# Latent norms inside the loop over tiles, and seven gate pairs a layer as block products with their last multiply on GpSimd

## The chip, the cores and the metric

The kernel runs on one core of one Trainium2 chip. The metric is device time in microseconds; the kernel before takes 1251.12 us (median of 3 runs, 1249.96 to 1251.63). A core has five engines with a queue each: TensorE (PE in the rows; its weight loads, PEld, run beside its matmuls), VectorE (DVE), ScalarE (ACT), GpSimd (POOL) and SyncE (SP), which here only issues DMA transfers.

## The reference

Two layers (DEPTH 2) on a sequence of 512 tokens of width 1024. A layer is a mixing part with four groups of attention heads, and a SwiGLU feed-forward part of inner width 2816:

```
z = rmsnorm(x, g_pre_mix) @ w_in                      # one projection for all four groups
z_moba, z_fox, z_fg, z_cq, z_ckv, z_kr, z_dil = split(z)
c_q  = rmsnorm(z_cq,  g_mla_q)                        # 192 wide   } the "latent norms"
c_kv = rmsnorm(z_ckv, g_mla_kv)                       # 128 wide   }
q_c = c_q @ w_mla_q_up ;  kv = c_kv @ w_mla_kv_up     # then rotary parts, attention
...                                                   # MoBA, FoX and dilated attention
x = x + rmsnorm(concat(heads) @ w_out, g_post_mix)
h = rmsnorm(x, g_pre_ffn)
f = silu(h @ w_gate) * (h @ w_up)
x = x + rmsnorm(f @ w_down, g_post_ffn)
```

All is float32. The kernel writes each operand as a sum of two parts (hi and lo), and one product is three matmuls (`mm3`: hi·hi, hi·lo, lo·hi, lines 197 to 199).

## The kernel before

Tokens are handled as four tiles of 128 (`NT`). The order of the instructions on each engine is set by the framework's scheduler from the order of the code, its dependences and its own costs; only the opening is written out by hand. Each engine then runs its list strictly in that order, and a list that waits holds up all that stands behind it. SP's list is the list of weight loads: each waits until one of five buffers `wraw` is free again.

**Start of the mixing part** (lines 540 to 665). A loop over the four tiles multiplies out the FoX values (`ps_v`) and the latent columns (`ps_lat`), and ScalarE copies the latter to `lat[t]` (L555). Then come FoX's q and k projections (`ps_qk`, 24 matmuls of 512 columns each). Only behind them in the code stand the gains' transfer (`gqkv`, L591 and L592, on SP's queue) and a second loop over the tiles with the latent norms: ScalarE sums the squares (L599, L600), GpSimd makes the factor r (L602 to L604), VectorE multiplies `lat` by r and gain (L605, L606), TensorE transposes three pieces (`cq0T`, `cq1T`, `ckvT`, L608 to L610). The transposed latents are split in hi and lo (`sp_hi`, `sp_lo`, L614, L615; `q_stk`, L620 and L621) and multiplied with the up weights, a tile at a time (`ps_qup`, `ps_kvup`), the results are put in natural order, and `natT` transposes them by heads (L670). `ps_cum` and `cumT` belong to FoX's forget gates, `ps_s` is a block of attention scores.

**Feed-forward part** (`ffn`). The 22 blocks j of 128 columns of w_gate and w_up are handled in pairs. Pair 0 is done in halves of the tokens. All ten other up pairs, and the gate pairs that start at j = 4, 8, 12, 16 and 20, go through `two_blocks`: the pair's weights as a 2 by 2 matrix of blocks, times h as a 2 by 2 matrix, in 7 products of blocks in place of 8. A product (`ps<-...`) is 12 matmuls of 256 columns, so a pair takes 84. It costs sums of weight blocks (`wsum`, `combine`, L886), a split of each sum or block (`whi` on ScalarE, `wlo` on VectorE, L880 and L881) and adds of the results (L898). The other gate pairs (2, 6, 10, 14, 18) are done directly (`ps_g`): 2 blocks of 24 matmuls of 512 columns, 48 in all, each block with two splits (L168, L173). When a pair's gate and up are there, silu (L936) and the multiply gate·up follow, in two instructions of 128x512 on VectorE (L944). Then f times w_down (`ps_d`) runs to the end of the layer.

Two names that the text uses: g4 is the gate pair that starts at block 4, u4 the up pair there.

Of the kernel before, what the change touches and what calls it, by code (L numbers as in the profile page):

```python
# [9 lines left out]
F32 = mybir.dt.float32  # L10
F32R = mybir.dt.float32r
I32 = mybir.dt.int32
AF = mybir.ActivationFunctionType
ALU = mybir.AluOpType
PSUM = bass.MemoryType.PSUM

P = 128
# [6 lines left out]
EPS = 1e-6  # L24
# [13 lines left out]
L_CQ, L_CKV, L_KR = 4, 196, 324  # L38
# [43 lines left out]
def decoder(ctx, tc, x, positions, w_in, b_forget, g_mla_q, w_mla_q_up, g_mla_kv, w_mla_kv_up,  # L82
            w_out, g_pre_mix, g_post_mix, w_gate, w_up, w_down, g_pre_ffn, g_post_ffn, consts, out):
    nc = tc.nc
# [4 lines left out]
    small = ctx.enter_context(tc.tile_pool(name="small", bufs=8))  # L89
# [5 lines left out]
    def bank(pool, name):  # L95
        return pool.tile([P, 512], F32, name=name, tag=pool.name)
# [4 lines left out]
    def R(dt, name):  # L101
        return keep.tile([P, 512], dt, name=name, tag="ring", bufs=NR)

    def T(dt, name):
        return keep.tile([P, 512], dt, name=name, tag="temp", bufs=NTMP)

    def H(name):
        return keep.tile([P, 512], F32, name=name, tag="part", bufs=NPART)
# [21 lines left out]
    mhalf = keep.tile([P, 2], F32, name="mhalf")  # L130
# [29 lines left out]
    def weights(src, shape, into=None):  # L160
        raw = wp.tile([P] + shape, F32, name="wraw", tag="wraw", bufs=WRAW)
        if into is None:
            hi = wp.tile([P] + shape, F32R, name="whi", tag="whi", bufs=WSPL)
            lo = wp.tile([P] + shape, F32R, name="wlo", tag="wlo", bufs=WSPL)
        else:
            hi, lo = into
        nc.sync.dma_start(raw, src)
        nc.scalar.copy(hi, raw)  # L168
        chunk_no[0] += 1
        if pool_share[0] and chunk_no[0] % pool_share[0] == 0:  # L170
            nc.gpsimd.tensor_tensor(lo, raw, f32(hi), op=ALU.subtract)
        else:
            nc.vector.tensor_tensor(lo, raw, f32(hi), op=ALU.subtract)  # L173
        return hi, lo
# [21 lines left out]
    def mm3(ps, a_hi, a_lo, b_hi, b_lo, start, stop):  # L196
        nc.tensor.matmul(ps, a_hi, b_hi, start=start, stop=False)  # L197
        nc.tensor.matmul(ps, a_hi, b_lo, start=False, stop=False)  # L198
        last_mm[0] = nc.tensor.matmul(ps, a_lo, b_hi, start=False, stop=stop)  # L199
# [74 lines left out]
    def mixing(l, h_in, in_slots, out_slots, w_first):  # L274
        def hh(k, ts=slice(0, S)):
            return h_in[0][k // 4][:, k % 4, ts]

        def hl(k, ts=slice(0, S)):
            return h_in[1][k // 4][:, k % 4, ts]
# [80 lines left out]
        def proj_qk(c0, rotary):  # L360

            passes = {}
            q = {}

            w = {}

            def fetch(j):
                w[j] = fetch_T(c0 + P * (2 * (j % 2) + j // 2))

            def step_q(i):  # L370
                ps = yield from proj_T(w[2 * i])
                q[i] = q_pair(rope(ps, 0.125), 1.0) if rotary else q_pair(ps, 0.125)

            def step_k(i):
                ps = yield from proj_T(w[2 * i + 1])
                for j, (kh, kl) in enumerate(k_pair(rope(ps, 1.0) if rotary else ps)):
                    passes[2 * i + j] = [(q[i][j], kh), (q[i][j], kl)]

            return passes, [(lambda j=j: fetch(j), lambda j=j: (step_k if j % 2 else step_q)(j // 2), 5.2) for j in range(4)]
# [156 lines left out]
        def window(col):  # L536
# [5 lines left out]
        lat = [latq[:, t, :] for t in range(NT)]  # L542
# [2 lines left out]
        lat_lo = [slot(s, F32R, "lat_lo") for s in out_slots[1:3]]  # L545
        wl = [weights(w_in[l, k * P:(k + 1) * P, C_LAT:C_LAT + N_LAT], [N_LAT],
                      into=(lat_hi[:, k, :], lat_lo[k // 4][:, k % 4, 0:N_LAT])) for k in range(KD)]
        for t in range(NT):
            for _ in steps[t][1]():
                pass  # L550
            ps = bank(ps_mm, "ps_lat")
            ts = slice(t * P, (t + 1) * P)
            for k in range(KD):
                mm3(ps[:, 0:N_LAT], hh(k, ts), hl(k, ts), *wl[k], k == 0, k == KD - 1)
            nc.scalar.copy(lat[t][:, 0:N_LAT], ps[:, 0:N_LAT])  # L555

        fox_passes, fox_qk = proj_qk(C_FOX, False)
        run(fox_qk[:1])
# [27 lines left out]
        if l == 0:  # L586
            with tc.issue_after(normed[0].ins), tc.issue_after(normed[1].ins):
                rope_tables()
        gains_lat = R(F32, "gqkv")
        gq, gkv = gains_lat[:, 0:192], gains_lat[:, 192:320]  # L590
        nc.sync.dma_start(gq, g_mla_q[l:l + 1, :].broadcast_to([P, 192]))  # L591
        nc.sync.dma_start(gkv, g_mla_kv[l:l + 1, :].broadcast_to([P, P]))  # L592
        jk = T(F32, "jk")
        pq0, pq1 = bank(ps_t, "cq0T"), bank(ps_t, "cq1T")
        pkv = bank(ps_s, "ckvT")
        for t in range(NT):
            ss = small.tile([P, 2], F32, name="ss2", tag="ss2")
            zq, zkv = lat[t][:, L_CQ:L_CKV], lat[t][:, L_CKV:L_KR]
            nc.scalar.activation(jk[:, 0:192], zq, AF.Square, accum_out=ss[:, 0:1])  # L599
            nc.scalar.activation(jk[:, 192:320], zkv, AF.Square, accum_out=ss[:, 1:2])  # L600
            r = small.tile([P, 2], F32, name="r2", tag="r2")
            nc.gpsimd.tensor_scalar(r[:, 0:1], ss[:, 0:1], 1.0 / 192, EPS, op0=ALU.mult, op1=ALU.add)  # L602
            nc.gpsimd.tensor_scalar(r[:, 1:2], ss[:, 1:2], 1.0 / 128, EPS, op0=ALU.mult, op1=ALU.add)
            nc.gpsimd.tensor_tensor(r, r, mhalf, op=ALU.pow)  # L604
            nc.vector.scalar_tensor_tensor(zq, zq, r[:, 0:1], gq, op0=ALU.mult, op1=ALU.mult)  # L605
            nc.vector.scalar_tensor_tensor(zkv, zkv, r[:, 1:2], gkv, op0=ALU.mult, op1=ALU.mult)  # L606
            ts = slice(t * P, (t + 1) * P)
            nc.tensor.transpose(pq0[:, ts], lat[t][:, L_CQ:L_CQ + P], ident)  # L608
            nc.tensor.transpose(pq1[0:64, ts], lat[t][:, L_CQ + P:L_CKV], ident)
            nc.tensor.transpose(pkv[:, ts], zkv, ident)  # L610
# [193 lines left out]
    def ffn(l, xt, h, turns, f_slots, after):  # L804
# [5 lines left out]
        def w_of(src, j, into=(None, None)):  # L810
            cs = slice(j * P, (j + 1) * P)
            return [weights(src[l, 4 * i * P:4 * (i + 1) * P, cs].rearrange("(k p) c -> p k c", p=P), [4, P], into=into[i])
                    for i in range(2)]
# [81 lines left out]
        def two_blocks(src, j, d1, d2):  # L895

            def add(to, a, b):
                nc.vector.tensor_tensor(to, a, b, op=ALU.add)  # L898

            c11, c12, c21, c22 = [d[:, s] for d in (d1, d2) for s in half]  # L900
            a11 = raw_of(src, j, 0)
            a21, a22 = raw_of(src, j + 1, 0), raw_of(src, j + 1, 1)
            a12 = raw_of(src, j, 1)
            p1 = product(ps_mm, split_w(a11), "11")
            nc.scalar.copy(c12, p1)
            s1 = combine(a21, a22, ALU.add)
            p5 = product(ps_s, split_w(s1), "T1")
            nc.scalar.copy(c22, p5)
            p2 = product(ps_o, split_w(a12), "21")
            add(c11, p2, c12)  # L910
            s2 = combine(s1, a11, ALU.subtract)
            p6 = product(ps_mm, split_w(s2), "T2")
            add(c12, p6, c12)
            s3 = combine(a11, a21, ALU.subtract)
            p7 = product(ps_t, split_w(s3), "T3")
            add(c21, p7, c12)
            s4 = combine(a12, s2, ALU.subtract)
            add(c12, c12, c22)
            add(c22, c22, c21)
            p3 = product(ps_s, split_w(s4), "22")  # L920
            add(c12, p3, c12)
            p4 = product(ps_t, split_w(a22), "T4")
            add(c21, p4, c21)

        for j in range(KF):
            if j < 2:
                (pg, _), (pu, _) = halves[2 * j:2 * j + 2]
            elif j - j % 2 in (4, 8, 12, 16, 20):
                if j % 2 == 0:
                    two_blocks(w_gate, j, fq[j], fq[j + 1])  # L930
                pg = fq[j]
            else:
                wg, pg = w_of(w_gate, j), bank(ps_mm, "ps_g")
                block(pg, wg, slice(0, 512))
            f = fq[j]
            nc.scalar.activation(f, pg, AF.Silu)  # L936
            if j < 2:
                nc.vector.tensor_tensor(f, f, pu, op=ALU.mult)
            elif j % 2 == 1:
                u = H("u1"), H("u2")  # L940
                two_blocks(w_up, j - 1, *u)
                for i in range(2):
                    f = fq[j - 1 + i]
                    nc.vector.tensor_tensor(f, f, u[i], op=ALU.mult)  # L944

        tail = 4
        gpost = gain(g_post_ffn, l)
# [20 lines left out]
        for t in range(NT):  # L968
# [4 lines left out]
            ss = small.tile([P, 2], F32, name="ssp", tag="ssp")  # L973
            for c in range(2):
                jk = T(F32, "jk3")
                square_mean(jk, acc[t][c], ss[:, c:c + 1])
                nc.vector.tensor_tensor(y[c], acc[t][c], gpost[c], op=ALU.mult)
            r = row_rstd(ss)
# [26 lines left out]
    with tc.manual_schedule(engines={mybir.EngineType.Activation, mybir.EngineType.DVE, mybir.EngineType.Pool}):  # L1005

        st, tr = {}, {}
        for o in "s0 a0 w0 w1 t0 s1 w2 w3 a1 s2 t1 a2 s3 t2 a3 t3".split():
            t = int(o[1])
# [50 lines left out]
```

## Time and profile before

| | |
|---|---|
| median of 3 runs | 1251.12 us |
| profiled execution: time / span | 1253.86 / 1252.0 us |
| TensorE busy | 1218.8 us (97%) |
| its weight loads | 1075.3 us (86%) |
| VectorE busy | 888.2 us (71%) |
| ScalarE busy | 667.4 us (53%) |
| GpSimd busy | 219.5 us (18%) |
| chain that ended last | TensorE 82%, VectorE 6%, ScalarE 4%, DMA 3% |
| granted TensorE clock | 0.995 |

How to read it: the profiled execution is one run of its own, 2.74 us above the median of the three. Matmuls are pipelined, so a matmul's row shows 0.28 us although the next starts 0.12 us after it; what a stretch of matmuls takes is read from start to start. The chain is followed backwards from the last instruction, at each step to what released it.

### The profile page before, as it was taken

How to read it: one execution, taken by the hardware profiler on the slowest of the kernel's cores; microseconds unless marked ns; L12 is line 12 of the kernel's file. 1: busy time of each engine (PE TensorE's matmuls, PEld its weight loads, DVE VectorE, ACT ScalarE, POOL GpSimd, SP SyncE). 2: the span in 40 equal slices, each digit the busy share in tenths (PEclk: the TensorE clock that was granted, in tenths of full speed). 3: DMA queues.
4: the chain of work that ended last, by engine and by line, in shares of the span. 5: the costliest groups of instructions: out<-in, count | busy, mean ns of one | idle time of the engine just before them, and what ended most of it. 6: DMA issues, size and time to landing. Idle time of an engine off the chain costs nothing.

```text
span 1252.0 us, 20776 instructions
## 1 busy us (share of the span) xinstructions
PE 1218.8 (97%) x7404; PEld 1075.3 (86%) x7404; DVE 888.2 (71%) x1801; ACT 667.4 (53%) x1453; POOL 219.5 (18%) x305
## 2 busy tenths in 40 slices
PE   8999999989999999999999999999999999999997
PEld 7878877779999999888787888778899999998886
DVE  6876877787988888533466778677789887893334
ACT  6676766754544445333356767576554544453332
POOL 3213334343000000000131324423430000000001
PEclk9999999999999999999999999999999999999999
DMA  7321242521433333433432222434223333333321
GB/s 230 75 60 43 63 122 65 166 68 35 120 102 108 104 108 93 136 93 101 133 112 74 59 57 65 107 94 135 68 60 111 116 104 110 103 110 118 95 93 73
DMA packets 158059, 121.67 MB, mean 97 GB/s; under 512 B 9090, under 2 KB 133122, under 8 KB 157956
## 3 DMA queue, kind: packets, MB, share of 16 engines
q1 hardware_dynamic: 151908, 111.55, 30.5%
q10 hardware_dynamic: 6048, 8.80, 2.6%
q8 instruction: 58, 0.95, 0.3%
q14 instruction: 45, 0.37, 0.1%
HBM read 111.93 MB, written 4.19 MB: 93 GB/s over the span
## 4 chain that ended last, share of the span: by engine, by line
PE 82%; DVE 6%; ACT 4%; DMA 3%; issue 2%; POOL 2%; ACTq 0%; SPq 0%; DVEq 0%; POOLq 0%
PE ps L197 8%; PE ps L199 8%; PE ps L198 8%; PE ps_d L197 6%; PE ps_d L198 6%; PE ps_d L199 6%; PE ps_g L198 4%; PE ps_g L197 3%; PE ps_g L199 3%; PE ps_s L454 3%; PE ps_qk L197 2%; PE ps_qk L199 2%; PE ps_qk L198 2%; PE pT L478 2%; PE ps_out L199 1%
## 5 line engine op out<-in xcount | busy, mean ns | idle before, releaser
L173 DVE TENSOR_TENSOR wlo<-wraw,whi 128x512 fp32r<-128x512 f32 x209 | 158.3, 766 | 133.2 <-ACT whi L168 131.1
L168 ACT CAST whi<-wraw 128x512 fp32r<-128x512 f32 (+1 forms) x228 | 138.5, 620 | 177.2 <-PE ps_d L199 121.0
L880 ACT CAST whi<-wsum 128x512 fp32r<-128x512 f32 x120 | 74.3, 620 | 133.4 <-DVE wsum L886 49.7
L197 PE MATMUL ps<-sum,whi 128*128 128x256 f32 x480 | 135.3, 282 | 0.0
L198 PE MATMUL ps<-sum,whi 128*128 128x256 f32 x480 | 135.2, 282 | 0.0
L199 PE MATMUL ps<-sum,wlo 128*128 128x256 f32 x480 | 135.1, 281 | 0.0
L240 POOL TENSOR_SCALAR rstd<-ssp 128x1 f32<-128x1 f32 x16 | 6.4, 398 | 641.6 <-ACT jk L236 641.5
L197 PE MATMUL ps_d<-whi,fh 128*128 128x512 f32 x288 | 112.2, 390 | 0.0
L199 PE MATMUL ps_d<-whi,fl 128*128 128x512 f32 x288 | 112.1, 389 | 0.0
L198 PE MATMUL ps_d<-wlo,fh 128*128 128x512 f32 x288 | 112.0, 389 | 0.0
L469 POOL TENSOR_SCALAR pr<-pr,den 128x128 f32<-128x128 f32 (+3 forms) x128 | 73.7, 591 | 188.2 <-DVE den L466 161.5
L199 PE MATMUL ps<-h,wlo 128*128 128x256 f32 x360 | 101.8, 283 | 0.0
L197 PE MATMUL ps<-h,whi 128*128 128x256 f32 x360 | 101.7, 282 | 0.0
L198 PE MATMUL ps<-h,whi 128*128 128x256 f32 x360 | 101.6, 282 | 0.0
L197 PEld LDWEIGHTS ps<-sum,whi 128*128 128x128 f32 x480 | 91.8, 191 | 0.0
L198 PEld LDWEIGHTS ps<-sum,whi 128*128 128x128 f32 x480 | 91.8, 191 | 0.0
L199 PEld LDWEIGHTS ps<-sum,wlo 128*128 128x128 f32 x480 | 91.7, 191 | 0.0
L198 PE MATMUL ps_g<-h,whi 128*128 128x512 f32 (+1 forms) x224 | 81.5, 364 | 5.8 <-DVE h L231 5.8
L881 DVE TENSOR_TENSOR wlo<-wsum,whi 128x512 fp32r<-128x512 f32 x120 | 80.9, 683 | 8.5 <-ACT whi L880 7.7
L197 PE MATMUL ps_g<-h,whi 128*128 128x512 f32 (+1 forms) x224 | 81.3, 363 | 1.0 <-ACT h L231 1.0
L199 PE MATMUL ps_g<-h,wlo 128*128 128x512 f32 (+1 forms) x224 | 81.0, 362 | 0.0
L880 ACT CAST whi<-wraw 128x512 fp32r<-128x512 f32 x90 | 55.8, 619 | 40.8 <-PE ps L198 28.1
(317 smaller groups left out, 3500.6 us busy)
## 6 DMA issues: line engine op xcount, KB each, us to landing
wraw<-in_w_gate_dram SPq DMA_DIRECT2D x88, 256.0 KB, 3.5
wraw<-in_w_up_dram SPq DMA_DIRECT2D x88, 256.0 KB, 3.1
wraw<-in_w_down_dram SPq DMA_DIRECT2D x88, 256.0 KB, 2.8
wraw<-in_w_in_dram SPq DMA_DIRECT2D x72, 256.0 KB, 3.1
wraw<-in_w_out_dram SPq DMA_DIRECT2D x32, 256.0 KB, 2.7
xt<-in_x_dram SPq DMA_DIRECT2D x16, 256.0 KB, 3.3
rope_b<-rope_a ACTq DMA_DIRECT2D x64, 64.0 KB, 2.0
wraw<-in_w_in_dram SPq DMA_DIRECT2D x16, 178.0 KB, 3.6
```

The costliest lines, as they stand in the source:

```text
L168: nc.scalar.copy(hi, raw)
L173: nc.vector.tensor_tensor(lo, raw, f32(hi), op=ALU.subtract)
L197: nc.tensor.matmul(ps, a_hi, b_hi, start=start, stop=False)
L198: nc.tensor.matmul(ps, a_hi, b_lo, start=False, stop=False)
L199: last_mm[0] = nc.tensor.matmul(ps, a_lo, b_hi, start=False, stop=stop)
L240: nc.gpsimd.tensor_scalar(r, ss[:, 0:1], ss[:, 1:2], EPS, op0=ALU.add, op1=ALU.add)
L454: nc.tensor.matmul(ps[:, 0:w], a if a.shape[-1] == P else a[:, qt * P:(qt + 1) * P], b[:, 0:w], start=i == 0, stop=i == n - 1)
L469: nc.gpsimd.tensor_scalar(p, p, den[:, t - qa:t - qa + 1], 1.0, op0=ALU.mult, op1=ALU.mult)
L478: nc.tensor.transpose(pt[:, i * P:(i + 1) * P], pr[:, offs[qt] + kt * P:offs[qt] + (kt + 1) * P], ident)
L880: nc.scalar.copy(hi, raw)
L881: nc.vector.tensor_tensor(lo, raw, f32(hi), op=ALU.subtract)
```

## The change

Two things. First, the transfer of the latent gains and the norms of a tile (squares, r, multiply) move from the second loop into the first, behind that tile's copy to `lat[t]`; the transposes stay where they were in the code. Second, the gate pairs done as products of blocks are now 4, 6, 10, 12, 16, 18 and 20 (direct are left 2, 8 and 14), and in these seven pairs GpSimd does the multiply gate·up in place of VectorE.

```diff
+        gains_lat = R(F32, "gqkv")
+        gq, gkv = gains_lat[:, 0:192], gains_lat[:, 192:320]
+        nc.sync.dma_start(gq, g_mla_q[l:l + 1, :].broadcast_to([P, 192]))
+        nc.sync.dma_start(gkv, g_mla_kv[l:l + 1, :].broadcast_to([P, P]))
+        jk = T(F32, "jk")
         for t in range(NT):
...
             nc.scalar.copy(lat[t][:, 0:N_LAT], ps[:, 0:N_LAT])
+            ss = small.tile([P, 2], F32, name="ss2", tag="ss2")
+            zq, zkv = lat[t][:, L_CQ:L_CKV], lat[t][:, L_CKV:L_KR]
+            nc.scalar.activation(jk[:, 0:192], zq, AF.Square, accum_out=ss[:, 0:1])
+            nc.scalar.activation(jk[:, 192:320], zkv, AF.Square, accum_out=ss[:, 1:2])
+            r = small.tile([P, 2], F32, name="r2", tag="r2")
+            nc.gpsimd.tensor_scalar(r[:, 0:1], ss[:, 0:1], 1.0 / 192, EPS, op0=ALU.mult, op1=ALU.add)
+            nc.gpsimd.tensor_scalar(r[:, 1:2], ss[:, 1:2], 1.0 / 128, EPS, op0=ALU.mult, op1=ALU.add)
+            nc.gpsimd.tensor_tensor(r, r, mhalf, op=ALU.pow)
+            nc.vector.scalar_tensor_tensor(zq, zq, r[:, 0:1], gq, op0=ALU.mult, op1=ALU.mult)
+            nc.vector.scalar_tensor_tensor(zkv, zkv, r[:, 1:2], gkv, op0=ALU.mult, op1=ALU.mult)
...
-            elif j - j % 2 in (4, 8, 12, 16, 20):
+            elif j - j % 2 in (4, 6, 10, 12, 16, 18, 20):
...
-                    nc.vector.tensor_tensor(f, f, u[i], op=ALU.mult)
+                    (nc.gpsimd if j - 1 in (4, 6, 10, 12, 16, 18, 20) else nc.vector).tensor_tensor(f, f, u[i], op=ALU.mult)
```

The same lines that are added to the first loop are removed from the second. The lists of the engines change as follows (line numbers behind the moved lines grow by one, or by their new place).

TensorE, layer 0, at the twelve transposes of the latents. Before, they stand near the end of FoX's k projection, three matmuls of it (`ps_qk`) still behind or between them:

```order
L199 MATMUL ps_qk<-h,wlo 128x512
L608 MATMUL cq0T<-cst,lat 128x128
L609 MATMUL cq1T<-cst,lat 64x128
L608 MATMUL cq0T<-cst,lat 128x128
L609 MATMUL cq1T<-cst,lat 64x128
L610 MATMUL ckvT<-cst,lat 128x128
L197 MATMUL ps_qk<-h,whi 128x512
L610 MATMUL ckvT<-cst,lat 128x128
L198 MATMUL ps_qk<-h,whi 128x512
```

Now, between the q projection's 24 matmuls and the k projection's 24:

```order
L199 MATMUL ps_qk<-h,wlo 128x512
L609 MATMUL cq0T<-cst,lat 128x128
L610 MATMUL cq1T<-cst,lat 64x128
L611 MATMUL ckvT<-cst,lat 128x128
L609 MATMUL cq0T<-cst,lat 128x128
L610 MATMUL cq1T<-cst,lat 64x128
L611 MATMUL ckvT<-cst,lat 128x128
```

All twelve transposes have moved ahead of the k projection; the first `ps_qup` stands right behind it. The place is the same in layer 1.

SP's list of transfers in layer 0; before, the gains come behind the weights of q, k and the up projections, and two of the loads of the next values:

```order
L167 DMA wraw<-in_w_in_dram 128x356 x3
L566 DMA bf<-in_b_forget_dram 128x4
L167 DMA wraw<-in_w_in_dram 128x356 x5
L167 DMA wraw<-in_w_in_dram 128x4x128 x4
L167 DMA wraw<-in_w_mla_q_up_dram 128x384
L182 DMA wraw<-in_w_mla_q_up_dram 64x384 x2
L167 DMA wraw<-in_w_mla_kv_up_dram 128x512
L167 DMA wraw<-in_w_in_dram 128x4x128 x4
L566 DMA bf<-in_b_forget_dram 128x4
L167 DMA wraw<-in_w_in_dram 128x2x256 x2
L591 DMA gqkv<-in_g_mla_q_dram 128x192
L592 DMA gqkv<-in_g_mla_kv_dram 128x128
```

Now:

```order
L167 DMA wraw<-in_w_in_dram 128x356 x3
L550 DMA gqkv<-in_g_mla_q_dram 128x192
L551 DMA gqkv<-in_g_mla_kv_dram 128x128
L581 DMA bf<-in_b_forget_dram 128x4
L167 DMA wraw<-in_w_in_dram 128x356 x5
L167 DMA wraw<-in_w_in_dram 128x4x128 x4
```

They moved ahead of five of the eight latent weight loads, in layer 1 to just behind the eighth.

GpSimd's list in the feed-forward part of layer 0; the first rows (`b`, sums of h) open that part, and before, the list then goes on with the norms at the end of the layer:

```order
L851 TENSOR_TENSOR b_3555<-h 128x512
L851 TENSOR_TENSOR b_3563<-h 128x512
L240 TENSOR_SCALAR rstd<-ssp 128x1
L241 TENSOR_TENSOR rstd<-rstd,mhalf 128x1
```

Now, with the multiplies of pair 4 (its up tiles are u_3942 and u_3943), pair 6 and so on between:

```order
L852 TENSOR_TENSOR b_3555<-h 128x512
L852 TENSOR_TENSOR b_3563<-h 128x512
L945 TENSOR_TENSOR f<-f,u_3942 128x512
L945 TENSOR_TENSOR f<-f,u_3943 128x512
L945 TENSOR_TENSOR f<-f,u_4236 128x512
L945 TENSOR_TENSOR f<-f,u_4237 128x512
```

Fourteen such rows stand there in each layer.

## Rows read from the trace of the kernel before

**Rows 1.** Page, part 1: busy us and share of each engine.

```profile
PE 1218.8 (97%) x7404; PEld 1075.3 (86%) x7404; DVE 888.2 (71%) x1801; ACT 667.4 (53%) x1453; POOL 219.5 (18%) x305
```

**Rows 2.** Stretches g6, then u6, g8, u8: start:end, length, busy us by engine, clock, DMA.

```profile
343.05:353.94 10.89, 10.89 (x50) 9.01 (x49) 7.54 (x14) 3.38 (x6) 0.00 (x0) 1.00 0.42 116
353.94:383.96 30.02, 30.02 (x254) 30.01 (x252) 26.36 (x52) 15.90 (x30) 0.00 (x0) 1.00 0.39 113
```

**Rows 3.** Timeline, TensorE, layer 0, from the latent projection to the transposes by heads.

```profile
23.83 0.43 PE L198 MATMUL ps_lat<-lat_lo,h 128*128 128x356 f32 x1 [0.26 <-DVE lat_lo L173]
...
48.01 0.39 PE L197 MATMUL ps_qk<-h,whi 128*128 128x512 f32 x1
...
53.59 0.33 PE L608 MATMUL cq0T<-cst,lat 128*128 128x128 f32 x1 [0.66 <-DVE lat L605]
...
55.70 0.27 PE L610 MATMUL ckvT<-cst,lat 128*128 128x128 f32 x1
55.81 0.29 PE L683 MATMUL ps_cum<-fg,cst 128*128 128x16 f32 x2
...
56.63 0.42 PE L197 MATMUL ps_qup<-whi,sp_hi 128*128 128x384 f32 x1
...
59.41 0.27 PE L691 MATMUL cumT<-cst,cpad 128*128 128x128 f32 x1
...
60.21 0.45 PE L197 MATMUL ps_qup<-whi,sp_hi 128*128 128x384 f32 x1
...
65.44 0.71 PE L670 MATMUL natT<-cst,nat 128*96 128x128 f32 x5
```

**Rows 4.** Timeline, VectorE: the first latent multiply, layer 0, then layer 1.

```profile
53.11 0.74 DVE L605 SCALAR_TENSOR_TENSOR lat<-lat,r,gqkv 128x192 f32<-128x192 f32 x2 [1.72 <-DMA gqkv<-in_g_mla_q_dram]
...
674.26 0.75 DVE L605 SCALAR_TENSOR_TENSOR lat<-lat,r,gqkv 128x192 f32<-128x192 f32 x2 [0.74 <-DMA gqkv<-in_g_mla_q_dram]
```

**Rows 5.** Timeline, SP: issues in the opening, then in layer 1.

```profile
10.61 0.42 SPq L566 DMA_DIRECT2D bf<-in_b_forget_dram  x1
12.83 10.96 SPq L167 DMA_DIRECT2D wraw<-in_w_in_dram  x9
...
659.84 11.29 SPq L167 DMA_DIRECT2D wraw<-in_w_in_dram  x6
671.17 0.46 SPq L591 DMA_DIRECT2D gqkv<-in_g_mla_q_dram  x1
```

**Rows 6.** Timeline, GpSimd, layer 0: the last tile's factor r.

```profile
44.52 0.69 POOL L604 TENSOR_TENSOR r<-r,mhalf 128x2 f32<-128x2 f32 x1
```

**Rows 7.** Timeline, VectorE, feed-forward: with GpSimd at work (two), then without.

```profile
299.62 0.69 DVE L938 TENSOR_TENSOR f<-f,ps_u 128x512 f32<-128x512 f32 x1 [0.19 <-ACT f L936]
...
307.22 1.78 DVE L886 TENSOR_TENSOR wsum<-wraw 128x512 f32<-128x512 f32 x1
...
327.62 1.28 DVE L944 TENSOR_TENSOR f<-f,u 128x512 f32<-128x512 f32 x2
```

**Rows 8.** Timeline, GpSimd, the same stretch.

```profile
298.91 1.68 POOL L851 TENSOR_TENSOR b<-h 128x512 f32<-128x512 f32 x1 [3.64 <-DVE sum L857]
...
304.21 4.24 POOL L851 TENSOR_TENSOR b<-h 128x512 f32<-128x512 f32 x3 [3.63 <-DVE sum L857]
```

**Rows 9.** Timeline, VectorE: splits of three weight blocks, in g4, u4 and g12.

```profile
328.82 0.68 DVE L881 TENSOR_TENSOR wlo<-wsum,whi 128x512 fp32r<-128x512 f32 x1
...
338.92 0.69 DVE L881 TENSOR_TENSOR wlo<-wraw,whi 128x512 fp32r<-128x512 f32 x1 [0.47 <-ACT whi L880]
...
407.71 1.28 DVE L881 TENSOR_TENSOR wlo<-wsum,whi 128x512 fp32r<-128x512 f32 x2
```

**Rows 10.** Timeline, TensorE: the first matmul of the products that use these splits.

```profile
330.23 0.28 PE L197 MATMUL ps<-h,whi 128*128 128x256 f32 x1
...
341.67 0.29 PE L197 MATMUL ps<-sum,whi 128*128 128x256 f32 x1
...
410.60 0.28 PE L197 MATMUL ps<-sum,whi 128*128 128x256 f32 x1
```

More of the change, by code (lines that the diff above doesn't have):

```diff
@@ L588, in mixing @@
                 rope_tables()
[L589 to L593, printed above, removed]
         pq0, pq1 = bank(ps_t, "cq0T"), bank(ps_t, "cq1T")
@@ L596, in mixing @@
         for t in range(NT):
[L597 to L606, printed above, removed]
+            zkv = lat[t][:, L_CKV:L_KR]
             ts = slice(t * P, (t + 1) * P)
```

## The prediction

> **What bounds the kernel now.** I read the page's busy times first: TensorE works 97% of the span, no other engine over 71% [rows 1]. The chain of waits puts 82% of the span on TensorE. So a part is worth what it takes from TensorE's list, or from TensorE's waits, and the views to read next are the two places that the change touches.
>
> In the feed-forward part, the busy times by stretch show TensorE without a gap: a direct gate pair takes 10.89 us, and the three products of a pair that follow it (u6, g8, u8) 30.02 us, all of it busy, its weight loads too (30.01), at a granted clock of 1.00 [rows 2]. VectorE is at 26.36 of 30.02 us there. TensorE sets the pace, VectorE is the next one behind it.
>
> In the mixing part, the timeline of TensorE in layer 0 shows the place where the latent norms hurt. FoX's k projection begins at 48.01, the transposes of the latents at 53.59 after a wait of 0.66 us for VectorE's multiply, the first tile's up products at 56.63, the second tile's at 60.21, the transposes by heads at 65.44 [rows 3]. VectorE's multiply itself waited for the gains' transfer, 1.72 us in layer 0 and 0.74 in layer 1 [rows 4]; SP issued it late, at 671.17 in layer 1, since the loads ahead of it in the list held SP for 11.29 us [rows 5]. The last tile's factor r was ready at 44.52 + 0.69 = 45.21 us [rows 6], eight microseconds before it was used.
>
> **The change part by part.**
>
> *Norms moved into the first loop.* Nothing is added or removed: the same 28 instructions a layer (for each of four tiles two squares, three steps of r, two multiplies) and the same two transfers stand earlier. What moves is the place of the twelve transposes, now ahead of the k projection. Its 24 matmuls then run while the latents are split, and what follows it finds its operands ready. I take the stretch from 48.01 to 65.44, 17.43 us [rows 3], and add up what it holds without the waits at the transposes and at the first tile: k projection 24 matmuls at the pitch of a direct gate pair (10.89/48 = 0.227 us [rows 2]) 5.44; twelve transposes at 55.81 - 55.70 = 0.11, 1.32; `ps_cum` 56.63 - 55.81 = 0.82; four tiles at the pace of the second to fourth, (65.44 - 60.21)/3 = 1.74, 6.97; `cumT` and the first four scores 60.21 - 59.41 = 0.80 [rows 3]. Sum 15.35, so 2.08 us a layer go, 4.2 us in both (layer 1 has the same pattern, its multiply waiting 0.74 us for the transfer). Bounds: at the most all that TensorE doesn't need would go; the pace of 1.74 has waits in it too, and if these went as well (a tile is five matmuls of 384 columns and three of 512, at the pitch above 5 x 0.17 + 3 x 0.227 = 1.53, so 0.21 less each) it would be 2.9 a layer. At the least nothing, if the attention behind it starts no earlier. I take 2.08, since the pace of the later tiles is set by ScalarE and PSUM, which the change doesn't touch.
>
> r is ready in time: at 45.21 against transposes that now stand at about 48.0 [rows 6, 3]; the two multiplies of a tile take about 0.7 us (half of 0.74 for the first of them, and about as much for the other) [rows 4]. The new wait is VectorE's, in the loop: each multiply waits there for r, and behind it stand the split of the next `ps_v` and, in layer 0, the rotary tables. Nobody needs these soon (the tables first serve MoBA's heads), and the values have three banks. I cost it at nothing; if the cover were gone, it is the 1.4 us of GpSimd's three steps, once a layer.
>
> The gains' two transfers now stand ahead of five latent weight loads. SP issues one in 0.42 us, so 0.84. SP stood idle from 11.03 to 12.83 there [rows 5], which hides the issue, but TensorE already waited 0.26 us for these weights at 23.83 [rows 3]. Between 0 and 0.84 in layer 0 alone; I take 0.4, the middle.
>
> *Two more gate pairs as products.* Pairs 6, 10 and 18 turn from direct to products and pair 8 the other way, so a layer has three direct pairs in place of five. A pair as products takes 30.02/3 = 10.01 us, a direct one 10.89 [rows 2], so 0.88 each, two a layer, four in all: 3.5 us. VectorE pays for it: three more splits, four sums and seven adds a pair. TensorE doesn't notice as long as they are done ahead of their product, which the next part weighs.
>
> A rule of the Trainium skill ("TensorE: Matmul & The Clock Gate", section "Back-to-back issue gap") gives the isolated gap between matmuls as columns over 2.4 plus 2.5 ns, about 109 ns at 256 columns. By that rule a pair of products would take 84 x 0.109 = 9.2 us and the four exchanges 7 us; the trace has 10.01 us with the weight loads busy all through [rows 2], and the measurement decides.
>
> *The multiply on GpSimd.* VectorE is freed of two instructions a pair, 1.28 us for both, starts 0.6 apart [rows 7], and GpSimd takes 4.24/3 = 1.41 for one of that size [rows 8]; GpSimd has nothing else to do in that stage, and f is needed only after the last pair. But VectorE is slowed: a sum of two operands in SBUF took 1.78 us while GpSimd ran such an instruction, 0.64 when GpSimd was idle (half of 1.28) [rows 7, 8], so 1.1 us are lost for each; an instruction with one operand in PSUM was not slowed (0.69 at 299.62, inside GpSimd's 298.91 to 300.59) [rows 7, 8]. Two multiplies on GpSimd so free VectorE of 1.2 us and cost it about 2.2, if it is always caught with two operands in SBUF, which 13 of its 18 instructions in a pair of products have; bounds 0 and 2.2.
>
> The Trainium skill's page "SBUF — State Buffer", section "Who interferes with whom", says it as a lock: a VectorE instruction with two SBUF inputs contends with a GpSimd instruction that reads SBUF, and the second to start blocks until the first is done. The trace agrees, with 1.78 beside 0.64 and the 0.69 of the one with a PSUM operand; taken at its word for every one of the 28 multiplies it gives the third rival below.
>
> Does that reach TensorE? The measure is by how much a split stands ahead of its product. In g4 the least is 330.23 - (328.82 + 0.68) = 0.73 us, at the end of u4 341.67 - (338.92 + 0.69) = 2.06, and in g12, after a direct pair had let VectorE catch up, 410.60 - (407.71 + 0.68) = 2.2 [rows 9, 10]. Each dip sits behind the two multiplies, 1.2 us of VectorE. In g6, now a pair of products, they cost 2.2 in place of 1.2: from a state like g4's the split comes 0.73 - 1.0 = 0.3 us too late. The lead of 2.06 with which g6 begins leaves little to catch that; with all of 2.2 against 0.73 it would be 1.5. So bounds are 0 and 1.5 us a layer; I take 0.6, nearer to the row's 0.3, and 1.2 for both layers. Later runs of products start behind a direct pair with a longer lead, and I cost them at nothing; if that cover is gone, it is the third rival.
>
> *Sum.* -4.2 + 0.4 - 3.5 + 1.2 = -6.1 us. On the profiled execution's 1253.86 us (span 1252.0 and 1.9 around it) that is 1247.8; that execution stands 2.74 us above the median of the runs, so 1245.0 us for a median.
>
> **The rivals.**
>
> *The port eats the exchange.* VectorE falls behind in the longer runs of products and TensorE waits as much as the exchange gave, 3.5 us. For it: VectorE is busy 26.36 of 30.02 us [rows 2], and each pair adds a net 1.0. Against: the leads of 2 us and more. Time 1251.1 - 4.2 + 0.4 = 1247.3.
>
> *The norms are hidden anyway.* The attention that follows starts no earlier, because its first scores wait for the forget gates' chain (`ps_cum`, `cumT`), which now stands later on TensorE. For it: `cumT` came at 59.41, before the second tile [rows 3], and it has been moved behind the tiles. Against: TensorE has projections to fill in there. Time 1251.1 - 3.5 + 1.2 + 0.4 = 1249.2.
>
> *VectorE becomes the bound, slower.* In the feed-forward stage each of the 28 multiplies blocks VectorE for 1.1 us, 30.8, and frees 0.6, 16.8; net 14.0, and TensorE follows VectorE there. It decides from the point where the lead of the splits is used up in all runs, not in g6 alone. Time 1251.1 + 14.0 - 3.5 - 3.8 = 1257.8. Against: it needs the whole lead gone, 2 to 10 us.
>
> **How the numbers follow.** Forecast 0.61 (1245.0, own range 1241.5 to 1247), the port eats the exchange 0.16, the norms hidden 0.13, VectorE the bound 0.06, and and 0.04 for all bounds won or more (no wait left at either place, -5.8 - 3.5 = -9.3, so 1241.8 or less). About 0.2%, 2.5 us, is what a measurement of this kernel can tell from no change, so faster means below 1248.6. The forecast, the first rival nearly whole and a third of the second are faster: 0.82; the rest of the second and a little of the others the same: 0.12; slower 0.06. Range for 8 in 10: 1241 to 1249.5, from all bounds won to the second rival.
>
> **What would show it.** Right: the direct pairs left are three a layer at 10.9 us and products still 10.0 without gaps over 0.2 us but in g6; the gains' transfer landing before the first multiply; twelve transposes at one pitch ahead of the k projection, the first `ps_qup` right behind it, and `natT` 2 us earlier against the start of k. VectorE's splits near 1.7 us wherever a GpSimd multiply runs. Wrong: TensorE waiting for `wlo` in g12 or g18; `natT` earlier but the first attention output not; `ps_lat` waiting a microsecond for its weights in the opening.

## The result: slower, 1269.1 us

After takes 1269.09 us (median of 4, 1267.29 to 1271.61) against 1251.02 of before in the same comparison, a ratio of 1.0149, 95% interval 1.0133 to 1.0166. Forecast was 1245.0, so the sign is wrong. The profiled span went from 1252.0 to 1268.0 us. The page of after, part 1, answers to [rows 1]:

```profile
PE 1218.6 (96%) x7548; PEld 1081.8 (85%) x7548; DVE 919.0 (72%) x1829; ACT 672.7 (53%) x1473; POOL 266.7 (21%) x333
```

TensorE's busy time is the same, so its idle time has grown by 16 us (33.2 to 49.4). A slower clock would not show there: it lengthens the busy time, from which four exchanges should have taken 3.5 us. So the places have to be found. The starts of the stages in TensorE's timelines (first matmul of gate pair 2, first `ps_d` of the down projection) cut the span into five (differences are taken before rounding):

| stretch | before | after | difference |
|---|---|---|---|
| start to gate pair 2, layer 0 | 302.1 | 298.9 | -3.3 |
| gate pair 2 to down projection, layer 0 | 204.6 | 213.1 | +8.6 |
| down projection, layer 0, to gate pair 2, layer 1 | 414.4 | 415.9 | +1.5 |
| gate pair 2 to down projection, layer 1 | 204.5 | 209.0 | +4.5 |
| down projection, layer 1, to the end | 126.4 | 131.2 | +4.8 |

The third row holds the norms of layer 1 as well, whose gain hides part of its loss.

**The norms did what was forecast.** TensorE's timeline of after in layer 0, answering to [rows 3]:

```profile
23.86 0.43 PE L198 MATMUL ps_lat<-lat_lo,h 128*128 128x356 f32 x1 [0.40 <-DVE lat_lo L173]
...
48.03 0.27 PE L609 MATMUL cq0T<-cst,lat 128*128 128x128 f32 x1
48.14 0.27 PE L610 MATMUL cq1T<-cst,lat 128*64 128x128 f32 x1
...
54.58 0.39 PE L199 MATMUL ps_qk<-h,wlo 128*128 128x512 f32 x1
54.80 0.34 PE L197 MATMUL ps_qup<-whi,sp_hi 128*128 128x384 f32 x1
...
62.80 0.49 PE L671 MATMUL natT<-cst,nat 128*96 128x128 f32 x3
```

The transposes run at one pitch without a wait, the first `ps_qup` stands right behind the k projection, and `natT` comes at 62.80 in place of 65.44. The opening's wait for weights grew by 0.14 us.

**The loss is at the end of each feed-forward part.** After has runs of five, five and seven sets of products (a set is the seven products of one pair) between direct pairs, before five runs of three. These are busy times of after in five stretches at the end of its last run and in one of the down projection behind it (us of PE, PEld, DVE, ACT, POOL, then the granted clock, DMA share, GB/s), answering to the second row of [rows 2]:

```profile
464.57:474.57 10.00, 10.00 (x86) 10.00 (x85) 10.00 (x17) 4.89 (x9) 3.00 (x2) 1.00 0.16 46
474.57:484.57 10.00, 7.90 (x64) 7.50 (x63) 6.61 (x14) 3.06 (x7) 0.00 (x0) 1.00 0.23 66
484.57:494.57 10.00, 8.77 (x74) 8.56 (x73) 8.21 (x16) 5.39 (x12) 1.50 (x2) 1.00 0.36 105
494.57:504.57 10.00, 9.63 (x79) 9.44 (x80) 9.12 (x17) 2.89 (x6) 1.45 (x1) 1.00 0.35 107
504.57:511.97 7.40, 4.89 (x42) 4.72 (x41) 6.94 (x14) 6.61 (x14) 0.00 (x0) 1.00 0.25 75
515.00:520.00 5.00, 5.00 (x13) 3.84 (x13) 0.83 (x1) 0.00 (x0) 1.97 (x2) 0.50 0.64 236
```

TensorE loses some 6 of the 37.4 us before 511.97. VectorE, for which it waits, is itself only 6.61 of 10 busy where TensorE first loses time (474.57 to 484.57): it waits as well. TensorE's waits in the feed-forward part of layer 0 of after (us in total, times, longest) name two places; in before it has none there:

```profile
PE ps L199 <- DVE wlo L882: 5.1, 6, 1.6
PE ps_d L197 <- DVE u L899: 4.2, 2, 2.5
```

The first is a split that comes after its product could have used it. The second is the handover: the down projection's sums take the banks of the last products, which VectorE's last additions must have emptied. There (504.57 to 511.97) VectorE is 6.94 of 7.40 us busy: its last additions stand in its list among the first splits of the down projection, so time that it lost before shows here. No run moved these splits. With the 6.4 us of the same two kinds in layer 1 this is 15.7 of the 16 us. TensorE's timeline at the handover:

```profile
511.97 0.47 PE L197 MATMUL ps_d<-whi,fh 128*128 128x512 f32 x1 [2.51 <-DVE u L899]
...
514.63 0.77 PE L197 MATMUL ps_d<-whi,fh 128*128 128x512 f32 x1 [1.72 <-DVE u L899]
515.20 0.63 PE L198 MATMUL ps_d<-wlo,fh 128*128 128x512 f32 x1
515.62 0.63 PE L199 MATMUL ps_d<-whi,fl 128*128 128x512 f32 x1
```

The last two stand 0.42 us apart, against 0.23 at the full clock: the granted clock stood at 0.50, the 1.2 GHz level, from 513.4 to 520.2 us. It fell inside the wait of 1.72 us, behind a stretch in which TensorE was busy 4.89 of 7.40 us. The thirteen matmuls from 514.63 to 520.28 take 5.65 us, some 2.7 more than at 0.23 each; this loss comes on top of the waits.

**Why VectorE waits.** Its timeline in the last run of after, then GpSimd's and SP's:

```profile
467.08 0.75 DVE L899 TENSOR_TENSOR u<-ps,u 128x256 f32<-128x256 f32 x2
467.74 3.45 DVE L882 TENSOR_TENSOR wlo<-wsum,whi 128x512 fp32r<-128x512 f32 x2
471.11 0.68 DVE L887 TENSOR_TENSOR wsum<-wraw 128x512 f32<-128x512 f32 x1
471.72 0.68 DVE L882 TENSOR_TENSOR wlo<-wraw,whi 128x512 fp32r<-128x512 f32 x1
...
472.92 0.68 DVE L882 TENSOR_TENSOR wlo<-wraw,whi 128x512 fp32r<-128x512 f32 x1
...
474.79 0.68 DVE L882 TENSOR_TENSOR wlo<-wraw,whi 128x512 fp32r<-128x512 f32 x1
478.86 0.69 DVE L887 TENSOR_TENSOR wsum<-wraw 128x512 f32<-128x512 f32 x1 [3.39 <-DMA wraw<-in_w_gate_dram]
```

```profile
467.64 3.00 POOL L945 TENSOR_TENSOR f<-f,u 128x512 f32<-128x512 f32 x2 [38.31 <-DVE u L899]
```

```profile
471.82 4.04 SPq L875 DMA_DIRECT2D wraw<-in_w_gate_dram  x4
```

Read it as a chain. Two splits take 3.45 us beside GpSimd's two multiplies, where they take 1.28 alone (482.34 in the same timeline). Behind them VectorE reads three weight blocks for the last time, in the sum at 471.11 and in the splits that end at 472.40 and 473.60. SP may load the next set only into buffers that are free, and issues its first three blocks right behind these ends, at 471.82, 472.42 and 473.63. The third lands at 478.78, and until then VectorE, at 475.47 through with all it had, waits 3.39 us for it. In e2 below, where VectorE multiplies, the same sum waits 0.40 us:

```profile
473.14 0.69 DVE L887 TENSOR_TENSOR wsum<-wraw 128x512 f32<-128x512 f32 x1 [0.40 <-DMA wraw<-in_w_gate_dram]
```

So what GpSimd takes from VectorE comes back a second time as a later load.

### The profile page after: what moved, and what is told of

The parts are those of the page before. It is cut to its first block, busy times and chain, and to the rows that moved or that the text cites. A ratio compares the mean times of both kernels' runs of the same rounds, so it can differ in the third digit from the quotient of the medians.

```text
span 1268.0 us, 21240 instructions
## 1 busy us (share of the span) xinstructions
PE 1218.6 (96%) x7548; PEld 1081.8 (85%) x7548; DVE 919.0 (72%) x1829; ACT 672.7 (53%) x1473; POOL 266.7 (21%) x333
## 4 chain that ended last, share of the span: by engine, by line
PE 65%; DVE 16%; issue 6%; ACT 5%; DMA 5%; POOL 3%; ACTq 0%; DVEq 0%; SPq 0%; POOLq 0%
PE ps_d L197 6%; PE ps_d L199 6%; PE ps_d L198 6%; PE ps L199 5%; PE ps L197 5%; PE ps L198 5%; DVE wlo L882 3%; PE ps_s L454 3%; PE ps_qk L197 2%; PE ps_qk L198 2%; PE ps_qk L199 2%; DVE wsum L887 2%; DMA wraw<-in_w_up_dram 2%; PE pT L478 2%; PE ps_g L198 2%
## 5 line engine op out<-in xcount | busy, mean ns | idle before, releaser
L168 ACT CAST whi<-wraw 128x512 fp32r<-128x512 f32 (+1 forms) x212 | 127.5, 620 | 163.8 <-PE ps_d L199 131.2
L199 PE MATMUL ps<-sum,wlo 128*128 128x256 f32 x544 | 154.0, 283 | 7.0 <-DVE wlo L882 7.0
L197 PE MATMUL ps<-sum,whi 128*128 128x256 f32 x544 | 153.4, 282 | 0.0
L198 PE MATMUL ps<-sum,whi 128*128 128x256 f32 x544 | 153.2, 282 | 0.0
L945 POOL TENSOR_TENSOR f<-f,u 128x512 f32<-128x512 f32 x28 | 43.9, 1584 | 375.6 <-DVE u L899 334.7
L199 PE MATMUL ps<-h,wlo 128*128 128x256 f32 x408 | 116.0, 284 | 0.3 <-DVE wlo L882 0.3
L197 PE MATMUL ps<-h,whi 128*128 128x256 f32 x408 | 115.2, 282 | 0.0
L198 PE MATMUL ps<-h,whi 128*128 128x256 f32 x408 | 115.1, 282 | 0.0
L882 DVE TENSOR_TENSOR wlo<-wsum,whi 128x512 fp32r<-128x512 f32 x136 | 110.1, 820 | 1.1 <-ACT whi L881 1.1
L197 PEld LDWEIGHTS ps<-sum,whi 128*128 128x128 f32 x544 | 104.0, 191 | 0.0
L198 PEld LDWEIGHTS ps<-sum,whi 128*128 128x128 f32 x544 | 104.0, 191 | 0.0
L199 PEld LDWEIGHTS ps<-h,wlo 128*128 128x128 f32 x408 | 77.9, 191 | 1.6 <-DVE wlo L882 1.5
L887 DVE TENSOR_TENSOR wsum<-wraw 128x512 f32<-128x512 f32 x68 | 51.4, 756 | 37.9 <-DMA wraw<-in_w_up_dram 21.5
L197 PEld LDWEIGHTS ps<-h,whi 128*128 128x128 f32 x408 | 77.9, 191 | 0.2
```

The lines of the kernel that those rows point to most:

```text
L887: nc.vector.tensor_tensor(s, a, b, op=op)
L945: (nc.gpsimd if j - 1 in (4, 6, 10, 12, 16, 18, 20) else nc.vector).tensor_tensor(f, f, u[i], op=ALU.mult)
```

## The experiments

The lead is, as in the prediction, the time by which a split ends ahead of the first matmul of its product. Theory A: GpSimd's multiplies block VectorE, and this uses up its lead. Theory B: a long run of products uses up the lead by itself, since VectorE waits in each set for blocks whose five buffers come free late; GpSimd only adds to it. All ran on `after` with the edits shown; ratios are to before.

**e1, the norms alone.**

```diff
-            elif j - j % 2 in (4, 6, 10, 12, 16, 18, 20):
+            elif j - j % 2 in (4, 8, 12, 16, 20):
...
-                    (nc.gpsimd if j - 1 in (4, 6, 10, 12, 16, 18, 20) else nc.vector).tensor_tensor(...)
+                    nc.vector.tensor_tensor(f, f, u[i], op=ALU.mult)
```

> The kernel before with the norms in the loop over tiles and nothing else: gates as products in pairs 4, 8, 12, 16 and 20, VectorE multiplying. In the trace of after the first direct gate pair begins at 298.85 us against 302.13 before, 3.28 us earlier, and layer 1 shows the same once the loss in the down projection is taken off. So both theories below expect 1251.1 - 2 x 3.3 = 1244.5 us, 1243.5 to 1245.5. If the gain came from something else than the norms (the other place of GpSimd's or SP's work), 1249 or more.

Measured 1246.69 us, ratio 0.9977 (0.9966 to 0.9988): 2.9 us gained, 1.5 to 4.3. The trace of after had made me expect 6.6; part of its early start was the clock, granted at 1.00 from 275 to 300 us there and at 0.93 in before.

**e2, seven pairs, VectorE multiplying.** The second of these edits alone.

> After, with VectorE doing all the multiplies of gate and up; seven gate pairs as products stay. Theory A (GpSimd's multiplies block VectorE, and that uses up its lead): the 14 multiplies a layer no longer block, so the lead holds and the time is 1251.1 - 6.6 - 3.5 = 1241 us, at most 1246. Theory B (a run of five or seven sets of products in a row uses up VectorE's lead by itself, since the first sum of a set waits 1.8 to 3.4 us for blocks whose five weight buffers come free only in the middle of the set before; GpSimd adds a little): TensorE still waits at the end of the last run and at the start of the down projection: 1255 to 1267.

Measured 1252.40, ratio 1.0022 (1.0011 to 1.0032). GpSimd's part in after is 16.7 us, yet the seven pairs still lose 5.7 to e1 where they should gain 3.5. The time lies between what the two theories had, so neither is enough alone: TensorE still waits 0.9 us for splits and 2.3 at the handover in layer 0.

**e3, the five pairs of before, GpSimd multiplying in them.** The first edit, and the same list in the second.

> The norms in the loop, the gate pairs of before (4, 8, 12, 16, 20) as products, and GpSimd multiplying gate and up in these five pairs. Theory A, in proportion to the multiplies (10 of 14 a layer, of some 28 us lost against the sum of the gains): 1244.5 + 20 = 1264 us, at least 1254. Theory B: runs of three sets never use up the lead, a direct pair restores it, so as with the norms alone: 1244.5 to 1247.5.

Measured 1247.43, ratio 0.9974 (0.9964 to 0.9983): 0.7 us over e1, inside the scatter, for ten multiplies a layer. In runs of three sets the multiplies cost TensorE nothing. A in proportion falls.

**e4, after with seven weight buffers for the products.** Two of the 24 blocks of the gate tiles hold no tile (there are 22), and take weights:

```diff
+        turn, spare = [0], [q.rearrange("p (k c) -> p k c", c=P) for q in fq[22:24]]
...
-            raw = wp.tile([P, 4, P], F32, name="wraw", tag="wraw", bufs=WRAW)
+            turn[0] += 1
+            raw = (spare[turn[0] % 7] if turn[0] % 7 < 2 else
+                   wp.tile([P, 4, P], F32, name="wraw", tag="wraw", bufs=WRAW))
```

> After, seven pairs and GpSimd multiplying, with seven weight buffers in place of five for the products (two blocks of the gate tiles' slots that hold nothing). Theory A: the blocked time stays, so 1269 within 4 us. Theory B: the blocks of the next set land before VectorE needs them, its waits for weights (21 us in the feed-forward part of layer 0) fall below 8 us, and the time is at most 1255.

Measured 1249.94, ratio 0.9999 (0.9988 to 1.0010): 19.2 us less than after, with every GpSimd multiply still there. VectorE's waits for weights in the feed-forward part of layer 0 (300 to 515 us), in after and then in e4:

```profile
DVE wsum L887 <- DMA wraw<-in_w_up_dram: 11.9, 8, 2.4
DVE wsum L887 <- DMA wraw<-in_w_gate_dram: 9.0, 5, 3.4
```

```profile
DVE wsum L891 <- DMA wraw<-in_w_up_dram: 4.1, 4, 1.5
```

One more wait of 2.4 us ahead of such a sum has no releaser in the profile; with it they are 6.5. TensorE waits for no split in e4. The edit also gives VectorE's list another order, in layer 0 alone. In layer 1, where the order is that of after, the time from gate pair 2 to the end is 331.4 us against 340.2, so the order alone doesn't explain the gain. What is left is the handover, 2.0 us in layer 0, and there the clock stays at 1.00: TensorE was busy 3.62 and 4.37 of 5.00 us from 500 to 505 and to 510.

**e5, both cures.** e4's buffers and VectorE multiplying.

> After, with both cures at once: seven weight buffers for the products and VectorE doing all multiplies. With after (1269.1), e2 (VectorE, five buffers: 1252.4) and e4 (GpSimd, seven buffers: 1249.9) it makes a table of two by two. Theory B (the two eat one lead, and TensorE only waits where it is gone): either cure alone is nearly enough, so this one gains little more, 1245 to 1249.5, the handover to the down projection being what is left. Theory A' (the two costs simply add up, 17 us for GpSimd and 19 for the buffers): 1269 - 17 - 19 = 1233, at most 1240.

Measured 1243.65, ratio 0.9944 (0.9930 to 0.9957), faster than both kernels. The table of medians:

| multiplies on | five buffers | seven buffers | buffers give |
|---|---|---|---|
| GpSimd | 1269.1 | 1249.9 | 19.2 |
| VectorE | 1252.4 | 1243.7 | 8.7 |
| VectorE gives | 16.7 | 6.2 | |

The two gains don't add up (1233 would be due): the two losses use up the same lead. VectorE waits for no block in e5's last run, and TensorE has no wait left in the feed-forward part: gate pair 2 to down projection takes 202.79 us in both layers, 1.76 under before's 204.55, which is two exchanges at 0.88 to the hundredth. The handover, now without a wait over 0.2 us:

```profile
500.85 0.39 PE L197 MATMUL ps_d<-whi,fh 128*128 128x512 f32 x1
501.08 0.40 PE L198 MATMUL ps_d<-wlo,fh 128*128 128x512 f32 x1
501.31 0.40 PE L199 MATMUL ps_d<-whi,fl 128*128 128x512 f32 x1
501.67 0.47 PE L197 MATMUL ps_d<-whi,fh 128*128 128x512 f32 x1
```

**e6, e7 and e8: six, seven and eight pairs spread, with e5's cures.**

```diff
+            elif j - j % 2 in (4, 8, 10, 14, 16, 20):              # e6
+            elif j - j % 2 in (4, 6, 8, 12, 14, 16, 20):           # e7
+            elif j - j % 2 in (4, 6, 8, 10, 12, 14, 16, 20):       # e8
```

> The norms in the loop, six gate pairs as products (4, 8, 10, 14, 16, 20) so that no run has more than five sets and a direct pair stands ahead of the last three sets, seven weight buffers, VectorE multiplying. Theory B (what is lost is lost at the end of long runs and in the handover to the down projection): each exchange gives 0.88 us and nothing is lost: 1246.7 - 1.8 = 1244.9 us, 1243.5 to 1246.5. Rival (a sixth pair of products costs VectorE more than it gives TensorE, wherever it stands): 1247 or more.

> As e6 with seven gate pairs as products (4, 6, 8, 12, 14, 16, 20): direct pairs at 2, 10 and 18, so two runs of seven sets, then a direct pair and three sets as before. Theory B: the down projection starts without a wait again, 1246.7 - 3.5 = 1243.2 us, 1242 to 1245.5. Rival (the number of pairs decides, not where the last direct one stands): as e4 and e5, above 1246.5.

> As e7 with eight gate pairs as products: direct pairs at 2 and 18 alone, one run of fifteen sets. With seven buffers VectorE has 8.95 us of sums, splits and additions in a set of 10.0, and 1.2 us of multiplies in every second one, so 0.4 us to spare in a set if it waits for no block: then 1246.7 - 5.3 = 1241.4 us, 1240 to 1244. Rival (VectorE still waits for blocks or for splits' buffers by more than 0.4 us a set, and the lead is used up in the long run): TensorE waits again, above 1246.

e6: 1248.35, ratio 0.9987 (0.9977 to 0.9997), a miss by 3.4 us. Its feed-forward part has the length expected (203.70 us, 0.85 under before) without a wait; what it lacks lies outside the products (of it 2.0 us from the down projection of layer 0 to gate pair 2 of layer 1, 411.3 against e1's 409.4) and stays open. e7: 1244.59, ratio 0.9950 (0.9937 to 0.9962), as e5. e8: 1245.40, ratio 0.9956 (0.9943 to 0.9969), a miss: its run of fifteen sets takes 151.2 us where 15 x 10.0 were due, so the eighth pair's gain (0.88) is lost in the run.

**e9, GpSimd in the first two runs alone.** After with `(4, 6, 10, 12)` as the list of the multiplies.

> After (seven pairs, five weight buffers), GpSimd multiplying in pairs 4, 6, 10 and 12 alone, VectorE in 16, 18 and 20. If GpSimd's multiplies cost in proportion to their number (4 of 7 pairs, of the 16.7 us between after and e2): 1252.4 + 9.5 = 1262 us. If they cost only where the splits' lead is used up, which in after is the last run (its gaps and the handover hold 8 of 9 us of TensorE's waits in layer 0, all in layer 1): 1252.4 to 1255.5.

Measured 1252.75, ratio 1.0018 (1.0006 to 1.0031), as e2. Eight of the 14 multiplies a layer cost 0.4 us in sum, inside the scatter; nearly all of the 16.7 comes with the six in the last run.

**e10, e7's pairs with the five buffers of before.**

> As e7 (seven pairs as products, direct pairs at 2, 10 and 18, VectorE multiplying), with the five weight buffers of before. If the run's length uses up the lead with five buffers, the two runs of seven sets show gaps of TensorE, 2 to 4 us a layer (the first begins with a lead of 0.5 to 3 us), but the down projection starts without a wait behind three sets: 1244.6 + 4 to 8 = 1248.5 to 1252.5 us. If e2's loss was the handover alone: 1244.6 to 1246.

Measured 1248.14, ratio 0.9982 (0.9972 to 0.9992), 0.4 us under the range of the first reading. The down projection starts without a wait again, and the runs of seven sets show TensorE's waits instead (layer 0, 300 to 516 us):

```profile
PE ps L199 <- DVE wlo L882: 2.0, 4, 1.1
```

So a direct pair ahead of the last three sets saves 4.3 us over e2, and the buffers are worth 3.6 to e7.

**e11, no multiply in the seven pairs.** They are left out, the rest as in after.

> After without the multiplies of gate and up in the seven pairs of products: they are left out, so the output is not the reference's. GpSimd blocks nothing and VectorE has 1.2 us a pair less to do than in e2. Theory B (VectorE's round of a set, its work and its wait for blocks, against TensorE's 10.0): 8.95 + about 1.0 of waiting = 9.95, so the lead just holds: 1243.5 to 1247. If the waits for blocks decide by themselves, whatever VectorE has to do, as e2: 1251 or more.

Measured 1251.70, ratio 1.0008 (0.9998 to 1.0019): no better than e2, though VectorE has 1.2 us a pair less to do. Theory B as I had put it (work and waiting add up to a round) falls; the time is that of the second reading. In the last run of layer 0 VectorE is busy 61.4 us, 3.2 less than in e2, and its waits show this work turned into waiting, for blocks (5.7 us against 4.5) and for ScalarE's halves of the splits (2.9 against 0.9):

```profile
DVE wsum L887 <- DMA wraw<-in_w_up_dram: 4.3, 3, 2.2
DVE wlo L882 <- ACT whi L881: 2.9, 3, 1.3
DVE wsum L887 <- DMA wraw<-in_w_gate_dram: 1.4, 1, 1.4
```

The least lead of a split over its product, taken from the two timelines for each gate set of the last run, goes 3.0, 2.1, 0.8 us in e11 and 2.8, 1.0, -0.3 in e2: about 1 us is lost in every two sets without any multiply, 1.5 with VectorE's; in after it goes 1.9, 0.6, -1.9. TensorE waits for no split in e11. What is left is the handover, 2.4 us in layer 0 and 2.2 in layer 1. So a long run on five buffers arrives there late by itself; how much of that is the loads alone e11 doesn't show.

**e12, eight pairs in two runs of nine sets, with e5's cures.** List `(4, 6, 8, 10, 14, 16, 18, 20)`.

> As e5 (seven weight buffers, VectorE multiplying) with eight gate pairs as products, direct pairs at 2 and 12, two runs of nine sets. If the lead holds over nine sets: 1243.65 - 1.8 = 1241.9 us, 1240.5 to 1243.5. If each further set in a run costs lead also with seven buffers (e8 lost about 1 us a layer in its run of fifteen): 1243.5 to 1247.

Measured 1244.14, ratio 0.9953 (0.9941 to 0.9966). Its feed-forward part is the shortest of all (201.88 and 202.03 us, no wait over 0.25), so the first reading's mechanism held, yet the whole is not to be told from e5 and misses its 1241.9. What e12 lacks lies outside the feed-forward parts and stays open.

## Why the prediction was wrong

- *Norms: right.* Forecast -3.8 us with the gains' transfers, e1 measured -2.9 (-4.3 to -1.5). The waits of VectorE for r that I cost at nothing (1.1 us in layer 0 of after) are not followed by a wait of TensorE for a split: its only wait from 24.2 to 66 us is one of 0.3 us for ScalarE's `qr`.
- *The exchange: right in size, 0.88 us a pair, where nothing waits* (e5: 1.76 a layer). In after none of it is seen, since the splits no longer keep pace.
- *The step that failed* is "Later runs of products start behind a direct pair with a longer lead, and I cost them at nothing". The lead is there at the start (9.0 us in the last run), and it is not held: it falls with every two sets, and after's last run has seven. The trace of before had this already. The prediction measured the lead in g4, u4 and g12, and not in the run of [rows 2] (u6, g8, u8), which stands behind a direct pair: there it goes from 9.2 us at the start of u6 to 369.70 - (368.35 + 0.68) = 0.67 in g8, sixteen microseconds later:

```profile
368.35 1.28 DVE L881 TENSOR_TENSOR wlo<-wsum,whi 128x512 fp32r<-128x512 f32 x2
...
369.70 0.28 PE L197 MATMUL ps<-sum,whi 128*128 128x256 f32 x1
```

  And VectorE's 26.36 busy us of 30.02 [rows 2] look like 3.7 to spare. The view of waits in the same stretch of before, which I did not weigh, says what those were:

```profile
DVE wsum L886 <- DMA wraw<-in_w_gate_dram: 3.0, 1, 3.0
DVE wsum L886 <- DMA wraw<-in_w_up_dram: 1.7, 1, 1.7
```

  4.7 us of waiting for weights (in part across the edges of the stretch): most of it was not spare, and the direct pair behind the run gave the lead back. So what a run costs by its length was left out of the sum. g6, for which I put 1.2 us in both layers, was sized about right (1.3 in layer 0, no wait in layer 1), but it was one of three places: the others are the end of the last run (u18 and g20) and the handover. The sign that I named, a wait for `wlo` in g12 or g18, would have missed them.
- *The multiply's price was about right, what it releases was not.* I gave 1.1 us lost and 0.6 freed for each. VectorE's splits of sums in layer 0, in after and then in e2 (busy us, mean ns):

```profile
L882 DVE TENSOR_TENSOR wlo<-wsum,whi 128x512 fp32r<-128x512 f32 x68 | 55.1, 820 | 0.5 <-ACT whi L881 0.5
```

```profile
L882 DVE TENSOR_TENSOR wlo<-wsum,whi 128x512 fp32r<-128x512 f32 x68 | 45.6, 682 | 0.7 <-ACT whi L881 0.6
```

  9.5 us more, and 2.4 in its sums (two rows of the same view), for 14 multiplies: 0.85 each, net 3.5 us a layer after the 8.4 freed. The Trainium skill's page "SBUF — State Buffer", section "Who interferes with whom", calls contention for the port pair that VectorE and GpSimd share an exclusive lock. The trace agrees: 3.45 us for two splits beside two multiplies. But 3.5 net became 8 us a layer (16.7 in both), because a blocked VectorE frees weight buffers late and delays the handover, and in both layers the clock fell there.
- *The third rival came nearest*, 1257.8 with a chance of 0.06. Its mechanism holds, its point of decision doesn't: the lead need not be gone in all runs (e9), the last one does it. Its price lacked the waits for blocks, the handover (2.5 + 1.7 us a layer) and the clock behind it (about 2.7 in layer 0, and as long at 0.50 in layer 1). That it came nearest is in part luck, since these terms were in no sum.

## What to carry to other kernels

Before an engine's idle time is counted as spare, ask the waits view what it waited for: a wait for loads whose buffers it frees itself is part of its round, and a longer run of the same work can use up a lead that is enough for a short one. When a step is moved to a slower engine that shares a path with the bound one's supplier, look at what the delayed supplier releases (buffers, banks), and put the relief where the run ends, before the next stage takes over. Try more buffers first: two free blocks of SBUF were worth 19 us here beside GpSimd's multiplies, 9 without them, and 4 where a direct pair stood ahead of the last three sets.

## What the hardware showed that I had not expected

- In both layers of after the granted clock fell to 0.50 (the 1.2 GHz level) inside the last of three waits of 1.6, 2.5 and 1.7 us within 20 us, and stayed there for 6.8 us; some 2.7 us were lost in layer 0. e4's two waits of 0.3 and 1.7 at the same place had no fall. The waits alone don't decide it: e11 has waits of 0.7 and 1.7 in layer 0 with a fall, e9 has 1.0, 0.6 and 1.7 in layer 1 without one. What decides is not shown.
- A single 256 KB load landed 2.8 to 5.1 us after its issue (median 3.1) in the stretch from 470 to 495 us of after, so a reader that has nothing else to do when its buffer comes free waits for the whole landing, 5.1 us behind the issue for the block that ended VectorE's 3.39 us wait.
